# A decoder trunk on one Trainium2 core: another beginning, paired row-half matmuls, and other settings of the planner that orders the program

## The chip, the core and the metric

One core of a Trainium2 chip runs the whole kernel: TensorE (PE) multiplies, VectorE (DVE) and ScalarE (ACT) work on tiles, GpSimd (POOL) does little here, and SyncE (SP) issues the transfers from and to the chip's memory. The metric is the device time of one launch in microseconds (us), the median of the runs.

## What is computed

Two layers, each with three mixers beside each other and a gated feed-forward part, on a sequence of 256 tokens of 1024 channels. All of it is in 32-bit floating point.

```python
c_act = jax.nn.silu(c)
for l in range(DEPTH):                                  # 2
    mod = c_act @ w_ada[l] + b_ada[l]                   # 1024 x 6144
    sh1, sc1, gt1, sh2, sc2, gt2 = jnp.split(mod, 6, axis=-1)
    h = modulate(rms_norm(x, norm_mix[l]), sh1, sc1)
    p = h @ w_in[l]
    y_att = dilated_mixture_attention(q, k, v)          # 8 heads of 64
    y_rwkv = rwkv7_time_mix(p[..., i0:i1], ...)         # 8 heads of 64, low-rank decay and a
    y_gmlp = chunked_spatial_gating(p[..., i1:i2], ...)
    gates = jax.nn.sigmoid(p[..., i2:].reshape(B, S, N_BRANCH, D))
    branch = jnp.einsum('bsnw,nwd->bsnd', ys, w_branch[l])
    x = x + gt1[:, None, :] * (jnp.sum(gates * branch, axis=2) @ w_out[l])
    h = modulate(rms_norm(x, norm_ffn[l]), sh2, sc2)
    x = x + gt2[:, None, :] * conv_gated_ffn(h, ...)
return rms_norm(x, norm_final)
```

## The kernel before

**Layout.** Channels lie on the 128 partitions, tokens in the free dimension: `x` is 128 x 8 x 256, eight tiles of 128 channels. Every wide matmul is done three times with operands split into a high part, rounded to a narrower form (`hhi`, `whi`), and a remainder (`hlo`, `wlo`): high by high, high by remainder, remainder by high. The weights come as a stream of chunks of 128 x 2048, in transfers of 1024 columns into the buffers `raw`; for each, one engine makes the high part (ACT or DVE, whichever the planner picks) and DVE subtracts it to get the remainder. `load` does this, `gemm2` and its relatives multiply with them.

**The projections of c.** Each needs 128 x 1024 weights (`wada`) multiplied by the row of c. DVE does most of them in one step with a running sum, against the row `crow`, which holds c on all partitions. Four in the beginning are done by PE, against the column `ccol` (`ada_col`; `ADA_ENG` says which).

**The beginning.** `setup` loads `x`, the row of c and the vectors `vec` (which hold the column of c too), computes the root mean square of `x` (`rstd`: squares on ACT, sums on PE, a power on POOL) and makes `crow`: a matmul with a row of ones spreads the row of c over the partitions, then tanh on ACT and two steps on DVE for each half of 512. `SEQ` lists the order of the first transfers: A is weights for c, W weights of the first `START` = 6 chunks, whose columns are laid out tile by tile. `norm_h` then makes the tiles of `hhi` and `hlo`, and `gemm_side` multiplies them tile by tile into six PSUM banks.

**The mixers.** `rwkv_half` does four RWKV heads; it begins with two low-rank products, of `th` (partitions 0 to 63 of `zx`) and `xa` (64 to 127), with `lora`. `head_rsqrt` then sums squares on PE (operand `tt`), takes a power of 8 columns on POOL (`rsqrt`), spreads it into `gt` and transposes it back on PE. `attention` does for each of four pairs of heads the scores, a softmax, a transpose and the product with the values. The scores of one head use partitions 0 to 63, those of the other 64 to 127. Its PSUM ring, `at`, has two banks.

**What sets the order.** Nothing is ordered by hand. Every operation is recorded with an engine (or two to choose from), an assumed duration and what it depends on; `Plan.flush` then schedules all of them on a model of the engines, forward and backward `ROUNDS` times, keeps the round with the earliest end, and emits the instructions in that order. Each engine runs its own list in order. `ORDER` fixes the order of the chunks in the stream. PSUM banks are taken in rings (`mm` with three, `rk` with three, `at` with two).

Of the kernel before, what the change touches and what calls it, by code (L numbers as in the profile page):

```python
# [15 lines left out]
OP = mybir.AluOpType  # L16
# [30 lines left out]
for _n, _w in (("ropec", 256), ("ropes", 256), ("abias", 384), ("mdiag", 64), ("moff", 64), ("mlow", 64),  # L47
# [9 lines left out]
    ("k0 r0 v0 u0 u1 t0 t1 g20 g21 g22 g23 p20 p21 q0 q1 k1 c0 c1 r1 v1 a0 a1 g00 g01 g02 g03 p00 p01 g10 "  # L57
# [28 lines left out]
class Plan:  # L86
# [11 lines left out]
    DMA_ISSUE = 1.1  # L98
    DMA_BW = 360e3
# [103 lines left out]
    def forward(self, prio):  # L203
# [18 lines left out]
        while todo:  # L222
# [26 lines left out]
            cost = o.alts[n][1]  # L249
            if len(o.alts) > 1:  # L250
# [11 lines left out]
            if e == "SP":  # L262
                free[e] = st + 0.5
                dma = o.end = max(dma, st + self.DMA_ISSUE) + cost
            elif e == "PE":
                free[e] = o.end = self.stream(st, cost, o.work)
            else:
                if e == "ACT" and o.table and o.table != table:
                    st, table = st + 1.28, o.table
                free[e] = o.end = st + cost  # L270
# [61 lines left out]
    def flush(self):  # L332
# [11 lines left out]
        best = None  # L344
        prio = [-o.cp for o in ops]
        self.log = []
        for k in range(ROUNDS):
# [5 lines left out]
            if k == ROUNDS - 2:  # L353
                for o, n in zip(ops, best[2]):
                    o.on = n
                ends = top
# [25 lines left out]
def decoder(ctx: ExitStack, tc: tile.TileContext, xT, crow_d, cst_d, vec_d, wada, stream, small, lnrow, bsrow, out):  # L382
# [28 lines left out]
    def pe(mms, main=False):  # L411
        cost, work, outs, ins, half = 0.0, 0.0, [], [], None
        for m in mms:
# [3 lines left out]
            was, half = half, (o.ap[0][1] == 64 and divmod(o.offset, o.ap[0][0])[0] or 0, o.ap[0][1] == 64)  # L417
            if was is not None and was[1] and half[1] and was[0] != half[0]:
# [5 lines left out]
            elif a.dtype == F32R:  # L424
                cost += max(_n(b) / 2400 + 0.0112, 0.112)
            else:
                cost += 2 * max(_n(b) / 1200 + 0.003, 0.1115)
# [182 lines left out]
    def load():  # L610
# [5 lines left out]
        for h in range(2):  # L616
# [4 lines left out]
            sub(lo, src, hi.bitcast(F32))  # L621
# [86 lines left out]
    def rsqrt(xc, y, t):  # L708
        P.add("POOL", 0.5, lambda: nc.gpsimd.tensor_tensor(y, xc, minus_half.to_broadcast(list(xc.shape)), op=OP.pow),  # L709
# [89 lines left out]
    def rwkv_half(l, hf, W, lora, th, xa, sg, yhi, ylo):  # L799
# [44 lines left out]
        pw = bank()  # L844
        pe([(bnc(pw, i), lora[0:64, (n0 + i) * 128:(n0 + i + 1) * 128], th[0:64, :], True, True) for i in range(2)])
        for i in range(2):
            act(sig[:, i, :], bnc(pw, i), AF.Tanh, scale=0.5, bias=dv[:, l, 14 + n0 + i:15 + n0 + i])
        ts(sig, sig, 0.5, 0.5, OP.mult, OP.add)
        pa = bank()
        pe([(bnc(pa, i), lora[64:128, (n0 + i) * 128:(n0 + i + 1) * 128], xa[64:128, :], True, True)  # L850
            for i in range(2)])
# [221 lines left out]
    def attention(l, W, yhi, ylo):  # L1073
# [120 lines left out]
    def setup(W):  # L1194
        tmp, wide2 = W["m3"], W["m2"]
        P.boost = 4000.0
        for j in range(4):
            dma(x[:, 2 * j:2 * j + 2, :], xT[:, 2 * j:2 * j + 2, :])
        dma(tmp[0:1, :], crow_d)
        dma(vec, vec_d)  # L1200
        memset(wide2[0:1, 0:128], 1.0)
        for n in range(2):
            ps = bank("mm")
            pe([(ps, wide2[0:1, 0:128], tmp[0:1, n * 512:(n + 1) * 512], True, True)])
            c = slice(n * 512, (n + 1) * 512)
# [6 lines left out]
        mul(ccol, tc, ccol)  # L1212
        for l in range(L):
# [272 lines left out]
def _pack(i):  # L1486
# [41 lines left out]
    return {"xT": xT, "crow": np.asarray(i["c"]), "cst": _constants(), "vec": vec, "wada": wada, "stream": stream, "small": small,  # L1528
# [19 lines left out]
```

## Time and profile before

| | |
|---|---|
| median of 3 runs | 1061.46 us (1059.19 to 1063.53) |
| the profiled execution | 1065.56 us |
| its span, first to last instruction | 1063.8 us |
| read from memory, written | 212.12 MB, 4.19 MB |
| mean rate over the span | 203 GB/s |
| granted TensorE clock, mean | 0.981 |

A profile row has a start, a duration, the engine, the line and the operation, then output<-inputs by the program's names, the shapes and a count; in brackets the idle time of the engine just before it and what ended that. Matmuls are pipelined: a row's duration is longer than the time until the next may start. A row that covers several instructions runs from the first one's start to the last one's end. A 32-bit matmul that isn't split stands as two records. In rows of waits the numbers are us in total, times, and the longest. In rows of stages: the stretch and its length, then busy us (instructions) of PE, weight load, DVE, ACT and POOL, the granted clock, the DMA engines' busy share and GB/s; where a view is of one engine, its columns alone.

### The profile page before, as it was taken

The page shows a single profiled execution, that of the slowest core. Times are in us where ns is not written, and L with a number is a line of the kernel's source. Part 1 is how long each engine was busy: PE and PEld are TensorE (multiplying, and loading weights), DVE is VectorE, ACT ScalarE, POOL GpSimd, SP SyncE. Part 2 cuts the span into 40 slices and gives each one's busy share as a digit, 9 for nine tenths or more (in the row PEclk, how much of TensorE's full clock was granted, in tenths as well). Part 3 has the DMA queues.
Part 4 walks back from the last instruction along what each step waited for, and adds up shares of the span by engine and source line. Part 5 has one row for each costly group of instructions (what it writes and reads, how often), then busy time and mean ns, then how long its engine had stood idle before and what let it go on. Part 6 is the DMA issues. An engine that isn't in the chain of part 4 may idle for free. (4 is left out here: it accounts for less than half of the span.)

```text
span 1063.8 us, 20460 instructions
## 1 busy us (share of the span) xinstructions
PE 1008.1 (95%) x8042; PEld 968.8 (91%) x8042; DVE 896.0 (84%) x1820; ACT 526.9 (50%) x917; POOL 34.4 (3%) x27
## 2 busy tenths in 40 slices
PE   5999998899999999999999999889999999999996
PEld 4989997689889999999999899879899999999996
DVE  6979999889769899999999799679976789877753
ACT  4364456656434555544436645455643465343341
POOL 0010000100000000000010100010000000000000
PEclk9999999899999899999999999999999999999998
DMA  9888565364578668988995454415434646555541
GB/s 350 322 279 264 190 210 185 118 203 162 186 257 275 201 218 299 315 287 279 380 314 191 146 163 138 157 34 182 134 118 136 217 143 207 190 181 187 185 143 40
DMA packets 70130, 217.65 MB, mean 205 GB/s; under 512 B 15121, under 2 KB 17169, under 8 KB 69522
## 3 DMA queue, kind: packets, MB, share of 16 engines
q1 hardware_dynamic: 70034, 216.35, 60.8%
q8 instruction: 63, 1.03, 0.4%
q14 instruction: 33, 0.27, 0.1%
HBM read 212.12 MB, written 4.19 MB: 203 GB/s over the span
## 5 line engine op out<-in xcount | busy, mean ns | idle before, releaser
L434 PE MATMUL bkm<-hhi,whi 128*128 128x256 f32 x1104 | 322.0, 292 | 5.2 <-DVE m L462 4.0
L462 DVE TENSOR_TENSOR wlo<-raw,whi 128x1024 fp32r<-128x1024 f32 x235 | 285.7, 1220 | 43.5 <-ACT whi L458 42.5
L434 PE MATMUL bkm<-hlo,whi 128*128 128x256 f32 x1104 | 314.5, 285 | 1.6 <-DVE hlo L495 1.6
L434 PE MATMUL bkm<-hhi,wlo 128*128 128x256 f32 x1104 | 314.0, 284 | 0.0
L458 ACT CAST whi<-raw 128x1024 fp32r<-128x1024 f32 x198 | 206.8, 1047 | 214.8 <-PE bkm L434 105.8
L434 PEld LDWEIGHTS bkm<-hhi,whi 128*128 128x128 f32 x1104 | 213.3, 193 | 11.8 <-issue 10.3
L434 PEld LDWEIGHTS bkm<-hlo,whi 128*128 128x128 f32 x1104 | 213.6, 193 | 2.4 <-DVE hlo L495 2.0
L434 PEld LDWEIGHTS bkm<-hhi,wlo 128*128 128x128 f32 x1104 | 213.4, 193 | 0.0
L434 PE MATMUL bkr<-hhi,whi 128*128 128x256 f32 x368 | 104.5, 284 | 0.0
L434 PE MATMUL bkr<-hlo,whi 128*128 128x256 f32 x368 | 104.5, 284 | 0.0
L434 PE MATMUL bkr<-hhi,wlo 128*128 128x256 f32 x368 | 104.4, 284 | 0.0
L434 PEld LDWEIGHTS bkr<-hhi,whi 128*128 128x128 f32 x368 | 71.1, 193 | 0.0
L434 PEld LDWEIGHTS bkr<-hlo,whi 128*128 128x128 f32 x368 | 71.0, 193 | 0.0
L434 PEld LDWEIGHTS bkr<-hhi,wlo 128*128 128x128 f32 x368 | 71.0, 193 | 0.0
L495 DVE SCALAR_TENSOR_TENSOR bd<-bd,crow 128x1024 f32<-128x1024 f32 x52 | 63.3, 1220 | 5.2 <-DMA bd<-in_wada_dram 5.0
L462 DVE TENSOR_TENSOR wlo<-m,whi 128x1024 fp32r<-128x1024 f32 x45 | 54.9, 1220 | 14.0 <-ACT whi L458 13.8
L458 ACT CAST whi<-m 128x1024 fp32r<-128x1024 f32 x39 | 40.8, 1047 | 49.2 <-PE bkm L434 23.3
L709 POOL TENSOR_TENSOR rs<-rs,vec 128x8 f32<-128x8 f32 (+2 forms) x17 | 23.4, 1377 | 766.8 <-DVE rs L482 668.6
L434 PE MATMUL bkm<-ygh,whi 128*128 128x256 f32 (+1 forms) x156 | 46.4, 298 | 0.6 <-ACT ygh L458 0.4
L434 PE MATMUL bkm<-ygl,whi 128*128 128x256 f32 x156 | 44.6, 286 | 1.7 <-DVE ygl L462 1.6
L434 PE MATMUL bkm<-ygh,wlo 128*128 128x256 f32 (+1 forms) x156 | 44.2, 284 | 0.0
L495 DVE SCALAR_TENSOR_TENSOR raw<-raw,crow 128x1024 f32<-128x1024 f32 x34 | 41.2, 1218 | 3.6 <-DMA raw<-in_wada_dram 3.6
(520 smaller groups left out, 2203.4 us busy)
## 6 DMA issues: line engine op xcount, KB each, us to landing
raw<-in_stream_dram SPq DMA_DIRECT2D x238, 512.0 KB, 4.7
bd<-in_wada_dram SPq DMA_DIRECT2D x52, 512.0 KB, 5.9
m<-in_stream_dram SPq DMA_DIRECT2D x47, 512.0 KB, 4.8
raw<-in_wada_dram SPq DMA_DIRECT2D x34, 512.0 KB, 5.1
m<-in_wada_dram SPq DMA_DIRECT2D x7, 512.0 KB, 8.7
scx<-x SPq DMA_DIRECT2D x2, 1024.0 KB, 10.0
x<-scx SPq DMA_DIRECT2D x2, 1024.0 KB, 7.0
x<-in_xT_dram SPq DMA_DIRECT2D x4, 256.0 KB, 4.2
```

The source lines that it names most:

```text
L434: nc.tensor.matmul(m[0], m[1], m[2], start=m[3], stop=m[4], skip_group_check=len(m) > 5)
L458: P.either([("ACT", _act(a), lambda: nc.scalar.copy(o, a)), ("DVE", 0.07 + _n(a) / (960 if _psum(o, a) else 1920), lambda: nc.vector.tenso ...
L462: P.add("DVE", 0.07 + _n(a) / 960, lambda: nc.vector.tensor_tensor(o, a, b, op=op), [o], [a, b])
L495: P.add("DVE", c, lambda: nc.vector.scalar_tensor_tensor(o, a, s, b, op0=op0, op1=op1, **k), [o, accum], ins)
L709: P.add("POOL", 0.5, lambda: nc.gpsimd.tensor_tensor(y, xc, minus_half.to_broadcast(list(xc.shape)), op=OP.pow), [y], [xc, minus_half])
```

## The change

The row of c is no longer loaded. The column of c goes through the same tanh form as before, and eight transposes of its entries, each spread over 128 columns, give the row, which is copied out of PSUM in two halves. `SEQ` is generated: for each channel tile its two A transfers, then the W transfers up to that tile. The two low-rank products of an RWKV half and the scores of two heads are recorded as one group each, with the two row halves in turn. The planner's settings: 100 rounds with random shifts of the end times instead of 12, other assumed costs for transfers, for matmuls of 64 rows, and for the power on POOL (0.6, 1.65 or 2.65 us by width instead of 0.5), and a rule by which DVE holds back an operation of over 0.5 us if a much more urgent one is ready within 0.15 us. The remainders of chunks 6 to 34 are made in halves of 512 columns. In layer 0, chunk g20 stands ahead of t0 and t1.

```diff
-    ("k0 r0 v0 u0 u1 t0 t1 g20 g21 g22 g23 p20 p21 q0 q1 k1 c0 c1 r1 v1 a0 a1 g00 g01 g02 g03 p00 p01 g10 "
+    ("k0 r0 v0 u0 u1 g20 t0 t1 g21 g22 g23 p20 p21 q0 q1 k1 c0 c1 r1 v1 a0 a1 g00 g01 g02 g03 p00 p01 g10 "
...
-SEQ = [(_a[0], int(_a[1]), int(_a[2])) for _a in (
-    "A01 W00 W01 A00 A10 A20 W10 W11 A21 A11 W20 A31 A30 A40 W21 A41 "
-    "A60 A51 A50 W30 W31 A61 W40 A71 W41 W50 W51 A70"
-).split()]
-ROUNDS = 12
+SEQ = []
+for _k in range(8):
+    SEQ += [("A", _k, 0), ("A", _k, 1)]
+    SEQ += [("W", _d // 2, _d % 2) for _d in range(-(-_k * START // 4), -(-(_k + 1) * START // 4))]
+ROUNDS, SEED = 100, 1
+FINE = 35
+HOLD, SHORT, WAIT, URGENT = ("DVE",), 0.5, 0.15, 10.0
...
-    DMA_ISSUE = 1.1
-    DMA_BW = 360e3
+    DMA_ISSUE = 1.75
+    DMA_BW = 340e3
...
+            if e in HOLD and cost > SHORT:
+                near = [x for x in w if not x[3].done and x[0] <= st + WAIT and prio[x[1]] < prio[o.i] - URGENT]
+                if near:
+                    heapq.heappush(a, (prio[o.i], o.i, n, o))
+                    free[e] = min(x[0] for x in near)
+                    continue
...
-                free[e] = st + 0.5
+                free[e] = st + 0.4
...
-            if k == ROUNDS - 2:
+            if k > 8:
                 for o, n in zip(ops, best[2]):
                     o.on = n
-                ends = top
+                s = (0.3, 1.0, 1.0, 3.0)[k % 4]
+                ends = [e + rng.gauss(0.0, s) for e in top]
...
-            was, half = half, (o.ap[0][1] == 64 and divmod(o.offset, o.ap[0][0])[0] or 0, o.ap[0][1] == 64)
-            if was is not None and was[1] and half[1] and was[0] != half[0]:
+            was, half = half, [(y.ap[0][1] == 64, divmod(y.offset, y.ap[0][0])[0]) for y in (o, a)]
+            if was is not None and any(p[0] and q[0] and p[1] != q[1] for p, q in zip(was, half)):
                 cost, half = cost + 0.035, None
...
-                cost += max(_n(b) / 2400 + 0.0112, 0.112)
+                cost += max(_n(b) / 2400 + 0.0125, 0.112)
...
-                cost += 2 * max(_n(b) / 1200 + 0.003, 0.1115)
+                cost += 2 * max(_n(b) / 1200 + 0.003, 0.1115) + (0.097 if a.ap[0][1] == 64 and _n(b) > 128 else 0.0)
...
-            sub(lo, src, hi.bitcast(F32))
+            for q in (slice(0, 512), slice(512, 1024)) if i < FINE else (slice(0, 1024),):
+                sub(lo[:, q], src[:, q], hi[:, q].bitcast(F32))
...
-        P.add("POOL", 0.5, lambda: nc.gpsimd.tensor_tensor(y, xc, minus_half.to_broadcast(list(xc.shape)), op=OP.pow),
+        P.add("POOL", {1: 0.6, 2: 1.65, 8: 2.65}[_n(xc)], lambda: nc.gpsimd.tensor_tensor(y, xc, minus_half.to_broadcast(list(xc.shape)), op=OP.pow),
...
-        pw = bank()
-        pe([(bnc(pw, i), lora[0:64, (n0 + i) * 128:(n0 + i + 1) * 128], th[0:64, :], True, True) for i in range(2)])
+        pw, pa = bank(), bank()
+        pe([(bnc(p, i), lora[h, (n0 + i) * 128:(n0 + i + 1) * 128], r[h, :], True, True)
+            for i in range(2) for p, h, r in ((pw, H[0], th), (pa, H[1], xa))])
...
-        pa = bank()
-        pe([(bnc(pa, i), lora[64:128, (n0 + i) * 128:(n0 + i + 1) * 128], xa[64:128, :], True, True)
-            for i in range(2)])
...
-            for hs in H:
-                ps = bank("at")
-                pe([(ps[:, 0:128], q[hs, n, 0:128], k[hs, n, 0:128], True, True),
-                    (ps[:, 128:384], q[hs, n, 128:256], k[hs, n, :], True, True)])
+            pss = [bank("at") for _ in H]
+            pe([x for c, kc in ((0, 128), (128, 256)) for ps, hs in zip(pss, H)
+                for x in [(ps[:, c:c + kc], q[hs, n, c:c + 128], k[hs, n, 0:kc], True, True)]])
+            for ps in pss:
...
+        dma(vec, vec_d)
         for j in range(4):
             dma(x[:, 2 * j:2 * j + 2, :], xT[:, 2 * j:2 * j + 2, :])
-        dma(tmp[0:1, :], crow_d)
-        dma(vec, vec_d)
-        memset(wide2[0:1, 0:128], 1.0)
-        for n in range(2):
-            ps = bank("mm")
-            pe([(ps, wide2[0:1, 0:128], tmp[0:1, n * 512:(n + 1) * 512], True, True)])
-            c = slice(n * 512, (n + 1) * 512)
-            act(crow[:, c], ps, AF.Tanh, scale=0.5)
-            ts(crow[:, c], crow[:, c], 1.0, 0.5, OP.add, OP.mult)
-            mul(crow[:, c], ps, crow[:, c])
...
         mul(ccol, tc, ccol)
+        for n in range(2):
+            ps = bank("mm")
+            pe([(ps[:, k * 128:(k + 1) * 128], ccol[:, 4 * n + k:4 * n + k + 1].to_broadcast([128, 128]), ident)
+                for k in range(4)])
+            acopy(crow[:, n * 512:(n + 1) * 512], ps)
```

Three places in the instructions' order follow, word for word, for PE. The first is its beginning, before: sq are squares of `x`, m_0 the row of c and the ones, vec holds the column of ones, the identity and the column of c, and VK and PB are here weights for c.

```order
L434 MATMUL bkm_93<-m_0_138,m_0_137 128x512
L434 MATMUL bkm_94<-m_0_138,m_0_137 128x512
L434 MATMUL bka_99<-vec,sq_108 128x1 x4
L434 MATMUL bka_99<-vec,sq_109 128x1 x2
L432 MATMUL bka_100<-vec,rs_90 128x128 x2
L434 MATMUL bka_99<-vec,VK_141 128x1 x8
L434 MATMUL bka_100<-vec,PB_140 128x1 x8
L434 MATMUL bkm_95<-hhi,whi_79 128x256
```

And with the change (m_115 are weights for c):

```order
L444 MATMUL bka_99<-vec,sq_108 128x1 x4
L442 MATMUL bkm_93<-vec 128x128 x4
L444 MATMUL bka_99<-vec,sq_109 128x1 x2
L442 MATMUL bkm_94<-vec 128x128 x4
L442 MATMUL bka_100<-vec,rs_90 128x128 x2
L444 MATMUL bka_99<-vec,m_115 128x1 x8
L444 MATMUL bka_100<-vec,VK_141 128x1 x8
L444 MATMUL bkm_94<-hhi,whi_79 128x256
```

The one-row matmuls are gone, the square sums stand first, and the eight transposes stand between them.

The second place is the start of the second RWKV half of layer 0, before: zx,lora are the low-rank products, tt the squares, gt what comes back from POOL.

```order
L434 MATMUL bka1_100<-m01_115 128x128
L434 MATMUL bka1_100<-m01_115 128x256
L432 MATMUL bkr0_96<-vec_66,kkn_1_156 128x128 x4
L434 MATMUL bkr2_98<-zx_1_158,lora_120 128x256 x2
L434 MATMUL bkr0_96<-cst_65,tt_1_157 128x2 x4
L432 MATMUL bkr1_97<-vec_66,gt_1_155 128x128 x4
L434 MATMUL bkm2_95<-whi2_81,hhi_75 128x512
```

With the change, its first rows:

```order
L444 MATMUL bkr1_97<-zx_1_158,lora_120 128x256
L444 MATMUL bkr2_98<-zx_1_158,lora_120 128x256
L444 MATMUL bkr1_97<-zx_1_158,lora_120 128x256
L444 MATMUL bkr2_98<-zx_1_158,lora_120 128x256
L444 MATMUL bkr0_96<-cst_65,tt_1_157 128x2 x4
L444 MATMUL bkm2_95<-hhi_75,whi1_80 128x256
L444 MATMUL bkm2_95<-hlo_76,whi1_80 128x256
L444 MATMUL bkm2_95<-hhi_75,wlo1_84 128x256
```

After 24 rows of wide matmuls of that kind (the last of them is the first row here) it goes on:

```order
L444 MATMUL bkm2_95<-hhi_75,wlo1_84 128x256
L442 MATMUL bka0_99<-vec_66,m3_0_138 128x128 x3
L442 MATMUL bka1_100<-vec_66,s21_1_160 128x128 x3
L442 MATMUL bkr1_97<-vec_66,gt_1_155 128x128 x4
L444 MATMUL bkm2_95<-whi2_81,hhi_75 128x512
```

Between the sums (tt) and the transposes (gt) there was nothing; now there are 24 wide matmuls and six transposes of the attention. The low-rank products, which stood in two groups apart, alternate between their two banks.

The third place is the same chain in the first RWKV half of layer 1, with the change:

```order
L444 MATMUL bkr1_97<-cst_65,tt_3_186 128x2 x4
L444 MATMUL bkm2_95<-hhi_75,whi0_79 128x256
L444 MATMUL bkm2_95<-hlo_76,whi0_79 128x256
L444 MATMUL bkm2_95<-hhi_75,wlo0_83 128x256
L444 MATMUL bkm2_95<-hhi_75,whi0_79 128x256
L444 MATMUL bkm2_95<-hlo_76,whi0_79 128x256
L444 MATMUL bkm2_95<-hhi_75,wlo0_83 128x256
L444 MATMUL bkm2_95<-hhi_75,whi0_79 128x256
L444 MATMUL bkm2_95<-hlo_76,whi0_79 128x256
L444 MATMUL bkm2_95<-hhi_75,wlo0_83 128x256
```

Three more wide matmuls follow and then the transposes of gt: 12 matmuls stand there now, where before 22 wide ones and four low-rank ones stood.

More of the change, by code (lines that the diff above doesn't have):

```diff
@@ L2 @@
 import math
+import random
 from contextlib import ExitStack
@@ L343, in flush @@
             o.cp = m + (o.cost + (self.DMA_ISSUE if o.eng == "SP" else 0.0)) * o.w + o.b
-        best = None
+        best, rng = None, random.Random(SEED)
         prio = [-o.cp for o in ops]
@@ L381, in decoder @@
 @with_exitstack
-def decoder(ctx: ExitStack, tc: tile.TileContext, xT, crow_d, cst_d, vec_d, wada, stream, small, lnrow, bsrow, out):
+def decoder(ctx: ExitStack, tc: tile.TileContext, xT, cst_d, vec_d, wada, stream, small, lnrow, bsrow, out):
     nc = tc.nc
@@ L1194, in setup @@
     def setup(W):
-        tmp, wide2 = W["m3"], W["m2"]
         P.boost = 4000.0
+        dma(vec, vec_d)
         for j in range(4):
             dma(x[:, 2 * j:2 * j + 2, :], xT[:, 2 * j:2 * j + 2, :])
-        dma(tmp[0:1, :], crow_d)
-        dma(vec, vec_d)
-        memset(wide2[0:1, 0:128], 1.0)
-        for n in range(2):
-            ps = bank("mm")
-            pe([(ps, wide2[0:1, 0:128], tmp[0:1, n * 512:(n + 1) * 512], True, True)])
-            c = slice(n * 512, (n + 1) * 512)
-            act(crow[:, c], ps, AF.Tanh, scale=0.5)
-            ts(crow[:, c], crow[:, c], 1.0, 0.5, OP.add, OP.mult)
-            mul(crow[:, c], ps, crow[:, c])
         tc = acol[:, 0:8]
@@ L1527, in _pack @@
     bsrow = np.ascontiguousarray(i["gmlp_b_s"])
-    return {"xT": xT, "crow": np.asarray(i["c"]), "cst": _constants(), "vec": vec, "wada": wada, "stream": stream, "small": small,
+    return {"xT": xT, "cst": _constants(), "vec": vec, "wada": wada, "stream": stream, "small": small,
             "lnrow": lnrow, "bsrow": bsrow}
```

## The prediction

> **What bounds the kernel now.** I read the engine table of the page first, then busy time by stage, then the list of waits of TensorE (PE), and then the order of time around the waits that the change touches.
>
> ```profile
> span 1063.8 us, 20460 instructions
> PE 1008.1 (95%) x8042; PEld 968.8 (91%) x8042; DVE 896.0 (84%) x1820; ACT 526.9 (50%) x917; POOL 34.4 (3%) x27
> ```
>
> The stages, by busy time of PE, weight load, VectorE (DVE), ScalarE (ACT) and GpSimd (POOL): the beginning, the mixers of layer 0, its feed-forward part, the same two of layer 1, and the end.
>
> ```profile
> 0.00:24.78 24.78, 13.57 (x51) 10.96 (x51) 16.23 (x47) 11.10 (x20) 1.88 (x5) 1.00 0.91 346
> 24.78:355.00 330.22, 307.02 (x2404) 288.88 (x2404) 287.95 (x624) 169.18 (x311) 14.76 (x9) 0.97 0.67 222
> 355.00:554.50 199.50, 198.03 (x1624) 197.83 (x1623) 194.23 (x372) 101.65 (x159) 4.32 (x3) 0.98 0.83 287
> 554.50:842.30 287.80, 276.32 (x2184) 258.34 (x2184) 237.11 (x514) 152.94 (x282) 12.05 (x9) 0.99 0.45 146
> 842.30:1054.50 212.20, 212.17 (x1779) 212.09 (x1779) 157.75 (x262) 91.55 (x146) 0.70 (x1) 1.00 0.51 167
> ```
>
> The feed-forward stages are solid PE (198.03 of 199.50, 212.17 of 212.20): nothing that moves other engines' work can shorten them, save for a reduced clock. 1779 matmuls in 212.2 us also give the price of one: 0.119 us. What can be won lies in the first 24.78 us and in the two mixer stages, where PE stands idle 23.2 us (330.22 - 307.02) and 11.5 us (287.80 - 276.32). DVE has 288 of 330 us there in layer 0, so it is the next bound. The idle spots have a second price:
>
> ```profile
> 201.07:211.30 10.23, 6.31 (x16) 0.50 0.32 103
> 166.90:170.30 3.40, 3.40 (x17) 0.50 0.50 144
> 354.70:364.90 10.20, 10.20 (x48) 0.50 0.72 242
> ```
>
> Behind some waits the granted clock is 0.50 for 3.4 or 10.2 us, and PE work in it counts half: 6.31 busy us cost about 3.2 us more than at full clock.
>
> **Part 1, the beginning.** Today's row of c comes by two one-row matmuls, tanh, and two DVE steps for each half:
>
> ```profile
> 7.56 3.75 PE L434 MATMUL bkm<-m,m 1*128 1x512 f32 x4 [7.56 <-DMA m<-in_crow_dram]
> 8.80 0.20 ACT L452 ACTIVATE acol<-vec 128x8 f32<-128x8 f32 x1
> 9.32 0.16 DVE L462 TENSOR_TENSOR vec<-acol,vec 128x8 f32<-128x8 f32 x1
> 9.63 0.60 ACT L452 ACTIVATE crow<-bkm 128x512 f32<-128x512 f32 x1 [0.63 <-PE bkm L434]
> 11.23 2.72 PE L434 MATMUL bka<-vec,sq 128*128 128x1 f32 x12
> 15.05 0.68 DVE L462 TENSOR_TENSOR crow<-bkm,crow 128x512 f32<-128x512 f32 x1
> 15.88 1.67 POOL L709 TENSOR_TENSOR rs<-rs,vec 128x2 f32<-128x2 f32 x1 [15.44 <-DVE rs L482]
> 17.61 0.69 PE L432 MATMUL bka<-vec,rs 128*128 128x128 f32 x2 [3.65 <-POOL rs L709]
> 18.09 3.41 PE L434 MATMUL bka<-vec,VK 128*128 128x1 f32 x16
> 21.36 3.55 PE L434 MATMUL bka<-vec,PB 128*128 128x1 f32 x16
> 24.78 0.56 PE L434 MATMUL bkm<-hhi,whi 128*128 128x256 f32 x1
> ```
>
> The row is whole at 15.73, and the square sums (vec,sq) stand behind the one-row matmuls on PE. The changed kernel needs the column of c, ready at 9.48 today (9.32 + 0.16). PE's rows are then four square sums, four transposes, two square sums, four transposes. A square sum is two of the twelve records, so 0.45 us (2.72 / 6): four take 1.8, from 8.85 (vec is there) to 10.65. A transpose costs 0.14 to 0.35 us (the pair at 17.61 took 0.69, PE took up the next work 0.48 after its start); at the small end, with a copy of 0.60 on ACT, the row is whole at about 13.5, 2.2 us sooner. The square sums end near 12; then DVE's short step, POOL 1.67, two transposes: about 14.9 instead of 18.3. PE next runs two projections of c (8 matmuls, 16 records, 3.41 us each), whose weights are the 11th and 13th of the transfers. The 13th is VK in both kernels and is there by 18.09 today, the 11th two transfers of 512 KB earlier; at the 408 GB/s below that is 2.6 us, so 15.5. PE: 15.5 to 18.9, then VK to 22.2, then the first projection matmul: **2.6 us** sooner than 24.78. DVE must have finished its first tile by then: from 13.5 the order gives it five steps of 1024 columns (1.2 us each) and shorter ones, 7 us together, 20.5, so it isn't late.
>
> ```profile
> 20.00:30.00 10.00, 10.00 (x48) 10.00 (x48) 9.86 (x21) 6.09 (x9) 0.00 (x0) 1.00 1.03 408
> ```
>
> Here PE (10.00), DVE (9.86) and the DMA engines (1.03) are all full. So an earlier start of PE counts as long as neither of the others makes it wait, and both do the same work as today. The transfers' new order on SP's queue moves no byte but the 4 KB of c, so the last weight lands as today. Bounds: 0, if a weight of the second or third tile is now the late one; 4, if the projections' weights are earlier than I infer.
>
> **Part 2, paired matmuls of 64 rows.** In the low-rank products (zx,lora) and the attention scores (bka<-m with 64 rows) the kernel multiplies one half of the partitions and then the other.
>
> ```profile
> 65.61 1.13 PE L434 MATMUL bkr<-zx,lora 64*128 64x256 f32 x4
> 66.67 1.05 PE L434 MATMUL bkr<-cst,tt 128*128 128x2 f32 x8
> 192.93 0.92 PE L434 MATMUL bka<-m 64*128 64x128 f32 x4
> 193.69 0.38 PE L434 MATMUL bkr<-zx,lora 64*128 64x256 f32 x1
> 223.64 0.27 PE L434 MATMUL bka<-s,m 128*64 128x128 f32 x1
> 223.64 0.27 PE L434 MATMUL bka<-m,m 128*64 128x128 f32 x1
> 223.75 0.27 PE L434 MATMUL bka<-s,m 128*64 128x128 f32 x1
> ```
>
> One group of the first kind holds PE for 1.06 us (65.61 to 66.67), one score group 0.76 (192.93 to 193.69). No row shows two halves of rows at once. Column halves do run together: the two at 223.64 start in the same hundredth, the next pair follows 0.11 later, the time of one. Bounds: 0 if row halves don't overlap, and 4 x 1.06 + 8 x 0.76 = 10.3 us if they do wholly (4 RWKV halves, 8 pairs of heads in two layers). I take the column pairs as nearest, and four fifths of it, **8.2**, since parts of the mixer stages are held by DVE.
>
> The Trainium skill, "TensorE: Matmul & The Clock Gate", part 3, says that matmuls in different row groups run at the same time; that would give the 10.3. Its "TensorEngine Tiling (Array Packing)", gotcha 1, speaks against: row tiles must not use one PSUM bank at once, so pairing costs banks. Here the scores of two heads take both banks of their ring together; no run yet shows the price.
>
> **Part 3, the new order around long chains.** In the chain behind the sums tt, POOL raises 8 columns to a power:
>
> ```profile
> 201.54 2.49 POOL L709 TENSOR_TENSOR rs<-rs,vec 128x8 f32<-128x8 f32 x1 [4.92 <-DVE rs L482]
> 204.06 0.62 ACT L458 COPY gt<-rs 128x512 f32<-128x512 f32 x1 [1.71 <-POOL rs L709]
> 204.73 1.12 PE L432 MATMUL bkr<-vec,gt 128*128 128x128 f32 x4 [3.97 <-ACT gt L458]
> PE bkr L432 <- ACT gt L458: 7.9, 3, 4.0
> PE bkr L432 <- DVE kkn L462: 1.9, 2, 1.7
> 354.56 0.72 PE L434 MATMUL bka<-vec,sq 128*128 128x1 f32 x3 [2.15 <-DVE sq L462]
> ```
>
> The planner counts 0.5 us for it now, 2.65 after the change. By the rows of the order, 11, 0, 26 and 18 wide matmuls stand between sums and transposes now (four low-rank ones among the 26); 58, 30 (six of them transposes), 12 and 42 after. The chain leaves PE 3.97 us with no cover. At 0.119 us, 58 and 42 cover it; 30 leave 0.4; 12 leave 2.5. So 7.9 us of idle time become 2.9: 5.0 gained. The second chain, to kkn, goes from 18, 36, 22 and 54 to 60, 48, 48 and 78: its 1.9 us become at most 0.2, 1.7 gained. With the 3.97 us goes most likely the half clock at 201.07 to 211.30, 3.2. Together **9.9**. At the end of the mixers of layer 0, six matmuls now stand ahead of vec,sq: **0.7** of the 2.15. The matmuls that cover are taken from elsewhere; where, no trace shows. I leave every other wait as it is; bounds -10 (new waits as long as those gone) and +14 (half of the other 25 us of mixer idle time goes too, and a little clock).
>
> **Part 4, remainders in halves.** 58 remainders of 1024 columns become 116 of 512.
>
> ```profile
> 45.16 0.68 DVE L462 TENSOR_TENSOR zr<-raw,zk 128x512 fp32r<-128x512 f32 x1
> 45.76 0.68 DVE L462 TENSOR_TENSOR aa<-raw,sig 128x512 fp32r<-128x512 f32 x1
> 47.05 1.23 DVE L462 TENSOR_TENSOR wlo<-raw,whi 128x1024 fp32r<-128x1024 f32 x1
> 48.20 1.22 DVE L462 TENSOR_TENSOR wlo<-m,whi 128x1024 fp32r<-128x1024 f32 x1
> ```
>
> By starts, two halves take 2 x 0.60 against 1.15: 0.05 more, 3 us in all; by durations 2 x 0.68 against 1.22: 0.14, 8 us. All of it falls in layer 0's mixers, where DVE is 87% busy. PE hides what it can as long as DVE isn't late; I take **-2** between 0 and -8. The gain is that PE may start on a first half 0.6 us earlier.
>
> **Sum.** 2.6 + 8.2 + 9.9 + 0.7 - 2 = 19.4 us. The profiled execution took 1065.56 (1063.8 of span, 1.8 around it): 1046.2. The median of the runs, 1061.46, is 4.1 lower, so the forecast is **1042**.
>
> **Rivals.**
> 1. The planner finds more: half of the other idle time goes too (+14) and pairs overlap wholly (+2): 1026. For it: waits of 4.03 and 2.04 us remain whose half clock would go with them. Against: DVE is at 87% and gets more work.
> 2. Pairing gives nothing: row halves run in turn, or the score groups wait for their two banks what they saved. 1042 + 8 = 1050. For it: the ring of the scores has two banks alone; against: the column pairs above, which gain in that ring.
> 3. The change doesn't do what it says in part 3: the cover is taken from places that then wait as long. Without 10.6 of the sum: 1053; with rival 2's loss too, 1061, no change.
> 4. Slower: DVE becomes the bound of layer 0's mixers and PE finds its PSUM banks not emptied, as once today:
>
> ```profile
> 166.78 0.42 PE L434 MATMUL bkm<-hhi,whi 128*128 128x256 f32 x1 [4.03 <-DVE m L462]
> ```
>
> That wait with its 3.4 us at half clock costs 4.03 + 1.7 = 5.7 us. Five new ones (28.5) outweigh the sum and give 1042 + 28.5 = 1071; from five on it is slower.
>
> **Chances.** Forecast 0.54 (1034 to 1048 by itself), rival 1 0.15, rival 2 0.11, rival 3 0.12 (half of it no change), rival 4 0.08. The range runs from 1024, below rival 1, to 1058, above 1053. A measurement of this kernel tells about 0.5% from no change: faster means below 1056, slower above 1067. Faster 0.54 + 0.15 + 0.11 + 0.06 = 0.86, the same 0.06, slower 0.08.
>
> **What would show it.** First hhi,whi matmul near 22 us; if it is at 24 or later, part 1 fell. Two zx,lora groups in about 1.1 us together instead of 2.1, and rows of both halves starting together; else part 2 fell. No wait on gt near the second RWKV half of layer 0 and clock 1.00 behind it, but one of 2 to 3 us in the first half of layer 1; else part 3 fell. Mixer stages of about 317 and 284 us (13 and 3.5 of the sum fall there). If the feed-forward stages change by more than 5 us, something is at work that I haven't seen.

## The result, and the profile after

The changed kernel takes 1034.17 us (median of 4 runs, 1032.91 to 1036.74) against 1061.83 for the kernel before in the same runs (1059.19 to 1063.53): the ratio is 0.9745, 95% interval [0.9715, 0.9774]. That is 27.7 us, where 19.4 were forecast. The engine table of the changed kernel's page:

```profile
span 1034.9 us, 20493 instructions
PE 987.6 (95%) x8046; PEld 954.2 (92%) x8046; DVE 905.1 (87%) x1911; ACT 517.2 (50%) x881; POOL 40.3 (4%) x27
```

For the stages, both kernels are now cut at two events that are in both: the first projection matmul, and the transposes that end the root mean square of `x` after each part. First the beginning, mixers, feed-forward part, mixers, feed-forward part of the kernel before; the columns are those of the stage rows above.

```profile
0.00:24.78 24.78, 13.57 (x51) 10.96 (x51) 16.23 (x47) 11.10 (x20) 1.88 (x5) 1.00 0.91 346
24.78:364.93 340.15, 316.95 (x2449) 298.81 (x2450) 296.17 (x637) 173.73 (x318) 16.38 (x10) 0.96 0.67 223
364.93:557.98 193.05, 191.58 (x1600) 191.38 (x1600) 188.47 (x365) 98.39 (x153) 4.32 (x3) 1.00 0.84 291
557.98:868.01 310.03, 298.55 (x2377) 280.57 (x2377) 254.28 (x542) 163.25 (x300) 11.13 (x8) 0.99 0.46 148
868.01:1056.41 188.40, 187.07 (x1570) 186.90 (x1568) 138.38 (x226) 80.12 (x127) 0.70 (x1) 1.00 0.49 160
```

The same view of the changed kernel:

```profile
0.00:23.66 23.66, 11.90 (x55) 11.16 (x55) 13.67 (x43) 9.04 (x18) 1.06 (x5) 1.00 0.90 338
23.66:344.97 321.31, 304.35 (x2449) 287.51 (x2450) 296.65 (x697) 172.73 (x313) 15.84 (x10) 0.99 0.70 233
344.97:537.13 192.16, 192.12 (x1613) 191.90 (x1612) 191.18 (x379) 91.26 (x132) 2.51 (x2) 1.00 0.83 284
537.13:839.89 302.76, 292.37 (x2372) 277.31 (x2371) 263.07 (x567) 163.55 (x291) 20.18 (x9) 0.98 0.51 162
839.89:1027.54 187.65, 186.32 (x1564) 186.15 (x1563) 138.04 (x224) 80.24 (x129) 0.69 (x1) 1.00 0.50 159
```

The beginning gives 1.1 us, the mixers of layer 0 18.8, those of layer 1 7.3, the two feed-forward parts 0.9 and 0.75. In layer 0 the granted clock tells most: 0.96 before, 0.99 after. Before, 27.3 us of that stage ran at half clock, and PE was busy in 23.4 of them; after, 3.4, all of them busy. If PE work at half clock counts half, that alone is 10.0 us. PE's idle time there fell from 23.2 (340.15 - 316.95) to 17.0, another 6.2, and the 2.6 that are left are less PE work. In layer 1 idle time gave 1.1 us (11.5 to 10.4) and the clock took 0.6 (4.9 to 6.1 busy us at half clock), so 6.8 us there are less PE work. Added up from the first projection matmul to the end of the last stage shown, in us:

| | PE's idle time | half of the busy time at half clock | PE work at full clock |
|---|---|---|---|
| before | 37.5 | 15.1 | 979.1 |
| changed kernel | 28.7 | 4.8 | 970.4 |

So 8.8 us came from idle time, 10.3 from the clock and 8.7 from less PE work.

The beginning, in order of time on PE in the changed kernel:

```profile
13.69 0.69 PE L442 MATMUL bka<-vec,rs 128*128 128x128 f32 x2 [0.24 <-POOL rs L720]
16.84 3.55 PE L444 MATMUL bka<-vec,m 128*128 128x1 f32 x16 [2.46 <-DMA m<-in_wada_dram]
20.24 3.55 PE L444 MATMUL bka<-vec,VK 128*128 128x1 f32 x16
23.66 0.56 PE L444 MATMUL bkm<-hhi,whi 128*128 128x256 f32 x1
```

The transposes of the root mean square come at 13.69 instead of 17.61, more than hoped for. Then PE waits 2.46 us for weights of c, which land at 16.84 and not at 15.5. What had been a wait for POOL is now a wait for a transfer.

The products of 64 rows, PE's groups by shape (busy us, mean ns of one), first before, then after:

```profile
L434 PE MATMUL bka<-m 64*128 64x256 f32 x32 | 9.5, 377 | 0.0
L434 PE MATMUL bkr<-zx,lora 64*128 64x256 f32 x32 | 8.9, 399 | 0.0
L434 PE MATMUL bka<-m 64*128 64x128 f32 x32 | 7.7, 319 | 0.5 <-DVE m L462 0.5
```

```profile
L444 PE MATMUL bka<-m 64*128 64x256 f32 x32 | 5.4, 382 | 0.0
L444 PE MATMUL bka<-m 64*128 64x128 f32 x32 | 4.7, 322 | 0.1
L444 PE MATMUL bkr<-zx,lora 64*128 64x256 f32 x32 | 4.5, 401 | 1.1 <-ACT hhi L468 1.1
```

One matmul takes as long as before, and the three rows' busy times add up to 26.1 us before and 14.6 after. The scores' two rows overlap a little, so some time is counted twice in that sum; the time in which any 64-row matmul runs falls from 23.2 to 12.7 us, by 10.5. The row halves do run beside each other.

PE's waits after the change, the longest groups among the mixers':

```profile
PE bkr L442 <- ACT gt L468: 6.1, 2, 4.1
PE bkr L442 <- DVE sig L472: 4.8, 2, 3.9
PE bkm L444 <- DVE hlo L472: 2.5, 2, 1.8
```

The waits on `gt` are one of 2.0 us in the second half of layer 0 and one of 4.1 in the first half of layer 1. The other two chain ends have no wait. The cover that was forecast (58, 30, 12 and 42 wide matmuls) is there, and two of four places wait, as forecast, but the second one for longer, for a reason that the section on the hardware looks into. The waits on `sig` stand under DVE, but most of the longest, 3.9 us, is a wait for a transfer, for which DVE itself waited:

```profile
152.71 0.69 DVE L472 TENSOR_TENSOR sig<-Tc,cst 128x512 f32<-128x512 f32 x1 [2.54 <-DMA Tc<-scb]
```

So not all of what the table below puts down to DVE is its own.

### The profile page after: what moved, and what is told of

Its sections match the earlier page's. It is cut to its first block, busy times and chain, and to the rows that moved or that the text cites. A ratio compares the mean times of both kernels' runs of the same rounds, so it can differ in the third digit from the quotient of the medians.

```text
span 1034.9 us, 20493 instructions
## 1 busy us (share of the span) xinstructions
PE 987.6 (95%) x8046; PEld 954.2 (92%) x8046; DVE 905.1 (87%) x1911; ACT 517.2 (50%) x881; POOL 40.3 (4%) x27
## 5 line engine op out<-in xcount | busy, mean ns | idle before, releaser
L468 ACT CAST whi<-raw 128x1024 fp32r<-128x1024 f32 x205 | 214.4, 1048 | 237.6 <-PE bkm L444 118.8
L472 DVE TENSOR_TENSOR wlo<-raw,whi 128x1024 fp32r<-128x1024 f32 (+1 forms) x293 | 293.0, 1008 | 33.9 <-ACT whi L468 32.5
L444 PEld LDWEIGHTS bkr<-hhi,wlo 128*128 128x128 f32 x368 | 70.6, 192 | 0.3 <-DVE wlo L472 0.3
L444 PEld LDWEIGHTS bkr<-hhi,whi 128*128 128x128 f32 x368 | 70.6, 192 | 0.0
L444 PEld LDWEIGHTS bkr<-hlo,whi 128*128 128x128 f32 x368 | 70.6, 192 | 0.0
L468 ACT CAST whi<-m 128x1024 fp32r<-128x1024 f32 x38 | 39.8, 1047 | 47.6 <-PE bkm L444 18.9
L720 POOL TENSOR_TENSOR rs<-rs,vec 128x8 f32<-128x8 f32 (+2 forms) x17 | 29.0, 1709 | 714.3 <-DVE rs L492 714.3
## 6 DMA issues: line engine op xcount, KB each, us to landing
m<-in_wada_dram SPq DMA_DIRECT2D x6, 512.0 KB, 10.2
```

What stands on the lines that cost most here:

```text
L444: nc.tensor.matmul(m[0], m[1], m[2], start=m[3], stop=m[4], skip_group_check=len(m) > 5)
L468: P.either([("ACT", _act(a), lambda: nc.scalar.copy(o, a)), ("DVE", 0.07 + _n(a) / (960 if _psum(o, a) else 1920), lambda: nc.vector.tenso ...
L472: P.add("DVE", 0.07 + _n(a) / 960, lambda: nc.vector.tensor_tensor(o, a, b, op=op), [o], [a, b])
L720: P.add("POOL", {1: 0.6, 2: 1.65, 8: 2.65}[_n(xc)], lambda: nc.gpsimd.tensor_tensor(y, xc, minus_half.to_broadcast(list(xc.shape)), op=OP. ...
```

## The experiments

Most edits are planned anew, so they also draw another order. The runs below give the size of that. Each ratio is to runs of the kernel before on the same chip; the kernels ran on several chips, so small differences between them are better read from the ratios. In the table, "PE waits" are the waits of PE after the first projection matmul, summed over the list of waits, with those that DVE ended in brackets; "half clock" is the time at 0.50 in the mixers and feed-forward stages; both are of one profiled execution, in us.

| kernel | median us | ratio to before, 95% interval | PE waits (on DVE) | half clock |
|---|---|---|---|---|
| before | 1061.83 | 1 | 37.0 (22.4) | 34.1 |
| before + pairs | 1059.18 | 0.9986 [0.9962, 1.0009] | 45.5 (29.9) | 30.7 |
| before + DVE's rule | 1060.16 | 0.9978 [0.9959, 0.9996] | 31.4 (20.9) | 30.7 |
| before + all settings | 1051.37 | 0.9905 [0.9874, 0.9936] | 28.9 (17.3) | 17.1 |
| before + all settings + pairs | 1034.68 | 0.9742 [0.9718, 0.9766] | 26.2 (17.5) | 17.4 |
| **changed kernel** | 1034.17 | 0.9745 [0.9715, 0.9774] | 27.2 (12.0) | 13.6 |
| halves of rows not in turn | 1035.23 | 0.9732 [0.9697, 0.9767] | 25.2 (12.8) | 20.4 |
| remainders whole | 1035.26 | 0.9733 [0.9699, 0.9766] | 28.3 (13.6) | 10.2 |
| POOL's cost 0.5 | 1038.93 | 0.9759 [0.9719, 0.9798] | 27.2 (13.3) | 6.9 |
| loop of 12 rounds | 1033.63 | 0.9734 [0.9679, 0.9790] | 24.7 (17.6) | 13.6 |
| pairs undone | 1037.64 | 0.9791 [0.9751, 0.9830] | 21.4 (10.2) | 10.2 |
| DVE's rule undone | 1047.29 | 0.9875 [0.9832, 0.9919] | 31.6 (23.0) | 30.7 |
| the same, another seed | 1045.33 | 0.9838 [0.9819, 0.9857] | 27.9 (15.4) | 17.1 |
| DVE's rule with 0.30 us | 1028.09 | 0.9679 [0.9657, 0.9701] | 18.3 (12.9) | 10.2 |

**Row halves one after the other.** The order of the plan stays; within each group the matmuls of the second half of rows come after those of the first.

```diff
+        seq = mms
+        if all(len(m) > 3 and m[1].ap[0][1] == 64 for m in mms):
+            seq = sorted(mms, key=lambda m: divmod(m[1].offset, m[1].ap[0][0])[0])
...
-            for m in mms:
+            for m in seq:
```

> The changed kernel with its order of instructions kept, but in each group of paired 64-row matmuls the one row half stands wholly before the other. Theory (the two halves overlap in full and TensorE sets the pace): the trace of the changed kernel has 0.97 us for a low-rank group of both halves and 0.76 us for a score group; in turn they take up to twice that, less one matmul that still overlaps where the halves meet, so 4 x 0.8 + 8 x 0.6 = 8 us more: 1042, all of it in the two mixer stages. Rival (the order has slack, or another engine sets the pace there): under 3 us more, 1037 or less.

1035.23, no change, but not for the reason given there. The first low-rank group in the order of time on PE, in this kernel:

```profile
67.39 1.14 PE L448 MATMUL bkr<-zx,lora 64*128 64x256 f32 x8
```

Its eight records take 1.14 us, as after the change, not twice as long. They start in twos, 13 ns apart, although the two of a pair stand four records apart in the program. So this edit took nothing away, and the run says nothing of what the overlap is worth. What brings the halves together again, the records, which don't name the half, don't show.

**Remainders whole.** The plan stays; the remainder of 1024 columns is made in one step at the place of the first half.

```diff
-                sub(lo[:, q], src[:, q], hi[:, q].bitcast(F32))
+                o = sub(lo[:, q], src[:, q], hi[:, q].bitcast(F32))
+                if i < FINE:
+                    o.alts[0] = ("DVE", o.alts[0][1], (lambda: None) if q.start else (
+                        lambda lo=lo, src=src, hi=hi: nc.vector.tensor_tensor(lo, src, hi.bitcast(F32), op=OP.subtract)))
```

> The changed kernel with its order kept, but each remainder of chunks 6 to 34 made in one piece of 1024 columns at the place of its first half. Theory (the halves cost VectorE 0.05 to 0.14 us each and win nothing that the trace shows): 0 to 3 us less, 1031 to 1034. Rival (TensorE really starts on first halves 0.6 us earlier, and waits without it): 2 to 6 us more, 1036 to 1040, with new waits of TensorE on wlo.

1035.26: the halves cost nothing and give nothing. DVE's groups by shape show the price that is hidden, 116 halves in the changed kernel, and the 58 whole remainders in this one (the third row):

```profile
L472 DVE TENSOR_TENSOR wlo<-raw,whi 128x1024 fp32r<-128x1024 f32 x177 | 215.3, 1220 | 30.0 <-ACT whi L468 29.0
L472 DVE TENSOR_TENSOR wlo<-raw,whi 128x512 fp32r<-128x512 f32 x116 | 77.7, 684 | 3.8 <-ACT whi L468 3.5
```

```profile
L635 DVE TENSOR_TENSOR wlo<-raw,whi 128x1024 fp32r<-128x1024 f32 x58 | 70.6, 1219 | 6.0 <-ACT whi L468 5.9
```

77.7 against 70.6 us of DVE, 7.1 more, and the mixers of layer 0 are not longer for it (321.31 against 320.11 whole). This kernel, the one before it and the changed kernel share one order, and yet have 10.2, 20.4 and 13.6 us at half clock: so much can differ between two executions of one order.

**POOL's power at the old cost.**

```diff
-        P.add("POOL", {1: 0.6, 2: 1.65, 8: 2.65}[_n(xc)], lambda: nc.gpsimd.tensor_tensor(y, xc, minus_half.to_broadcast(list(xc.shape)), op=OP.pow),
+        P.add("POOL", 0.5, lambda: nc.gpsimd.tensor_tensor(y, xc, minus_half.to_broadcast(list(xc.shape)), op=OP.pow),
```

> The changed kernel planned with the old duration of 0.5 us for the power on GpSimd. Theory (the honest duration is what put cover behind the sums): the cover falls below 34 matmuls at several of the four places, TensorE waits there 2 to 4 us each and gets half clock behind some: 6 to 12 us more, 1040 to 1046. Rival (the many rounds of the search matter, not this number): within 3 us of the changed kernel.

1038.93; its interval overlaps that of the changed kernel, and its profiled span is 1032.9. All four chain ends wait again (1.2, 2.6, 1.2 and 1.6 us on `gt`), so the cost does what it says there, but the whole hardly moves: 1.5 us by the ratios, as the rival has it.

**The old loop of 12 rounds.**

```diff
-ROUNDS, SEED = 100, 1
+ROUNDS, SEED = 12, 1
...
-            if k > 8:
+            if k == ROUNDS - 2:
...
-                s = (0.3, 1.0, 1.0, 3.0)[k % 4]
-                ends = [e + rng.gauss(0.0, s) for e in top]
+                ends = top
```

> The changed kernel planned with the old loop: 12 rounds and no random shifts; costs, pairs and the beginning as changed. Theory (costs and pairs matter most): 2 to 8 us more, 1036 to 1042. Rival (the search itself is the larger part of the gain): 10 us more or beyond, 1044 and up.

1033.63: the longer search is worth nothing that shows. The orders of the last two runs and that of the changed kernel (which the first two runs share) end between 1033.6 and 1038.9, so 5 us is what a newly drawn order may do at the least, and less than that can't be put down to an edit here.

**Pairs undone.** Each half of rows is a group again.

```diff
-        pw, pa = bank(), bank()
-        pe([(bnc(p, i), lora[h, (n0 + i) * 128:(n0 + i + 1) * 128], r[h, :], True, True)
-            for i in range(2) for p, h, r in ((pw, H[0], th), (pa, H[1], xa))])
+        pw = bank()
+        pe([(bnc(pw, i), lora[0:64, (n0 + i) * 128:(n0 + i + 1) * 128], th[0:64, :], True, True) for i in range(2)])
...
-            pss = [bank("at") for _ in H]
...
+            for hs in H:
+                ps = bank("at")
...
```

> The changed kernel with the low-rank products and the scores recorded as before, each row half as a group of its own (one PSUM bank of the scores' ring at a time). Theory P (the two row halves side by side are worth 8 to 10 us, as forecast): 1042 to 1045 us, 8 to 10 above the changed kernel, and the mixers of layer 0 and 1 longer by about 5 and 4. Theory S (the scheduler's settings carry the gain, the pairs little): 1034 to 1038.

1037.64, in the range of theory S. The time of the groups is back, by shape:

```profile
L444 PE MATMUL bka<-m 64*128 64x256 f32 x32 | 9.5, 377 | 0.0
L444 PE MATMUL bkr<-zx,lora 64*128 64x256 f32 x32 | 9.0, 401 | 0.4 <-ACT zx L462 0.4
L444 PE MATMUL bka<-m 64*128 64x128 f32 x32 | 7.8, 322 | 0.2 <-DVE m L505 0.2
```

26.3 us instead of 14.6. But this order has 5.8 us fewer waits (21.4 against 27.2) and starts its first projection matmul at 19.4, with one of the projections of c (3.4 us) put behind it. So 11.7 us of PE work show as 3.5 us of time (4.9 by the ratios), within what a new order may do.

**DVE's rule undone.**

```diff
-HOLD, SHORT, WAIT, URGENT = ("DVE",), 0.5, 0.15, 10.0
+HOLD, SHORT, WAIT, URGENT = (), 0.5, 0.15, 10.0
```

> The changed kernel without the rule by which DVE holds back a long operation for a more urgent one. Theory H (the rule carries a third or more of the 27 us): 1043 us or more, with new waits of PE on short DVE steps (kkn, s, sq) in the mixers of layer 0. Theory P or S without it: 1032 to 1037, within the scatter of a re-drawn order.

1047.29: 13 us, the largest of all single edits. That is theory H's number, but the longest waits are not those it named. The waits of PE on DVE:

```profile
PE bkr L442 <- DVE sig L472: 9.8, 4, 4.5
...
PE bkr L444 <- DVE BK L472: 2.4, 2, 1.8
...
PE bkr L442 <- DVE yrh L472: 1.8, 1, 1.8
...
PE bkm L444 <- DVE zv L505: 1.5, 1, 1.5
```

And its mixers of layer 0, with two of the stretches at half clock in them:

```profile
24.27:357.30 333.03, 312.00 (x2455) 294.75 (x2456) 299.09 (x709) 172.67 (x312) 19.55 (x10) 0.96 0.68 227
...
164.92:175.16 10.24, 8.69 (x54) 7.33 (x52) 10.05 (x22) 4.52 (x10) 0.00 (x0) 0.50 0.48 155
199.05:209.29 10.24, 8.78 (x30) 6.66 (x30) 9.88 (x23) 4.28 (x11) 1.69 (x1) 0.50 0.34 116
```

The stage is 11.7 us longer than after the change, at the old granted clock of 0.96: 4.1 us more idle time, 10.4 more for the clock (24.3 busy us at half clock against 3.4) and 2.8 less PE work. The waits on DVE are 23.0 us instead of 12.0, as many as before the change (22.4); all waits together rise by 4.4.

**Pairs alone, and the settings alone**, on the kernel before; the lines are those of the change's diff, of which a few are shown. Pairs:

```diff
-            was, half = half, (o.ap[0][1] == 64 and divmod(o.offset, o.ap[0][0])[0] or 0, o.ap[0][1] == 64)
+            was, half = half, [(y.ap[0][1] == 64, divmod(y.offset, y.ap[0][0])[0]) for y in (o, a)]
...
+        pw, pa = bank(), bank()
...
+            pss = [bank("at") for _ in H]
...
```

> The kernel before with the pairs alone, and the planner's recognition of them. Theory P: 1052 to 1054, 8 to 10 below the kernel before. Theory S: 1059 to 1063, the same as before. Theory X: 1056 to 1062, since the old costs leave the idle spots where they are.

Settings, with the costs of matmuls of 64 rows and of POOL's power:

```diff
-ROUNDS = 12
+ROUNDS, SEED = 100, 1
+HOLD, SHORT, WAIT, URGENT = ("DVE",), 0.5, 0.15, 10.0
...
-    DMA_ISSUE = 1.1
-    DMA_BW = 360e3
+    DMA_ISSUE = 1.75
+    DMA_BW = 340e3
...
```

> The kernel before with the planner's settings alone (100 rounds, the rule for DVE, the costs of transfers, of matmuls of 64 rows and of POOL's power); beginning, chunk order, pairs and remainders as before. Theory S (settings carry the gain): 1036 to 1044, 18 to 26 below the kernel before. Theory P (pairs carry 8 to 10, the settings about 10 as forecast): 1050 to 1053. Theory X (it is the pieces together, none alone): 1056 or more.

The pairs alone leave the time where it was, 0.9986 [0.9962, 1.0009]: their groups fall from 26.1 to 16.4 us, and PE's waits rise from 37.0 to 45.5. The settings alone give 0.9905 [0.9874, 0.9936], some 10 us.

**Settings and pairs together, and DVE's rule alone**, on the kernel before (the first has the edits of both runs above, the second only the line with HOLD and the rule).

> The kernel before with the planner's settings and the pairs; beginning, chunk order and remainders as before. If the two add up (work -9 by the pairs, losses -14 by the settings): 1040 to 1043, work 994, and the beginning and g20 are worth the other 6 to 8. If the rest of the change is worth no more than its first matmul (about 1): 1033 to 1037. If the pairs gain nothing on this base, as nearly on the old one: 1048 to 1052.

> The kernel before with DVE's rule alone (12 rounds, old costs, no pairs). So far PE's full-clock work (span less idle time less half of the half-clock time) is 1002 to 1004 without pairs and 992 to 994 with them, and idle plus lost clock is 61 before, 42 after, 54 after without the rule. Theory H (the rule by itself keeps PE from waiting): 1048 to 1052, losses near 49, work 1003. Rival C (the rule works only with the right costs): 1058 to 1063, losses 57 or more.

Together they give all of it: 0.9742 [0.9718, 0.9766], against 0.9745 [0.9715, 0.9774] for the whole change. The first projection matmul is at 25.06 in that kernel, 1.4 us later than after the change, and the end is the same; on top of the settings and the pairs, the new beginning, g20 and the halves add nothing that can be measured. The pairs gain 16.7 us on the settings, where they gained next to nothing without them. But the changed kernel with its pairs undone, which has the settings and these three pieces, ends 13.7 us below the settings alone (1037.64 against 1051.37, on the same chip). Either the pieces count where the pairs are missing, or one of these two orders is an uncommon draw, and then a new draw can do far more than 5 us; no run decides it. So 16.7 is no price of the pairs.

What the pairs do in every order is to take PE work away. Reckoned at full clock as in the table of the result, it is 967 to 973 us in the ten kernels with pairs, and 979 to 981 in the four without (where a projection of c stands behind the first projection matmul, its 3.4 us are taken off). The settings act on the rest: idle time and clock, 52.6 us before, are 37.7 with the settings alone, 34.4 with the pairs too and 33.5 after the change.

DVE's rule alone gives 0.9978 [0.9959, 0.9996], some 2 us: its worth also hangs on the rest.

**DVE's rule undone, from another seed.**

```diff
-ROUNDS, SEED = 100, 1
+ROUNDS, SEED = 100, 2
...
-HOLD, SHORT, WAIT, URGENT = ("DVE",), 0.5, 0.15, 10.0
+HOLD, SHORT, WAIT, URGENT = (), 0.5, 0.15, 10.0
```

> The changed kernel without DVE's rule, as e8, from another seed: another draw of the order. Theory H (the rule is worth about 12): 1042 to 1050. Rival D (e8 was an unlucky draw): 1033 to 1038, as the four orders with the rule.

1045.33: two orders without the rule at 1045 and 1047, four with it and with the pairs at 1034 to 1039 (the changed kernel, POOL's cost 0.5, 12 rounds, settings and pairs). The rule is the likely cause of the 11 to 13 us between them (10 to 14 by the ratios), but with 1051 for the settings alone, which have the rule, two unlucky draws can't be ruled out. Where this second order loses it is less plain than in the first: its waits are 27.9 us, like the changed kernel's, of them 15.4 on DVE, where settings and pairs have 17.5 with the rule, and its half clock is 17.1. One thing both share: POOL's first power of 8 columns, which the first RWKV half of layer 0 needs, starts at 74.05 and 73.79 us, and at 63.4 to 69.6 in every order with the rule.

**The rule with 0.30 us instead of 0.15.**

```diff
-HOLD, SHORT, WAIT, URGENT = ("DVE",), 0.5, 0.15, 10.0
+HOLD, SHORT, WAIT, URGENT = ("DVE",), 0.5, 0.3, 10.0
```

> The changed kernel with DVE holding a long step back for an urgent one that is ready within 0.30 us instead of 0.15. Theory H: the same or a little less, 1028 to 1036, losses 38 to 42. Rival (0.15 just hit a good order): 1038 or more.

1028.09 (1027.80 to 1029.13), ratio 0.9679 [0.9657, 0.9701], clear of the changed kernel's interval (each against the kernel before, on other chips): this version beats both. Its page, and its two mixer stages:

```profile
span 1025.9 us, 20483 instructions
PE 987.3 (96%) x8046; PEld 954.2 (93%) x8046; DVE 896.6 (87%) x1894; ACT 523.0 (51%) x898; POOL 34.3 (3%) x27
```

```profile
24.99:342.43 317.44, 306.55 (x2455) 290.45 (x2456) 294.01 (x695) 173.84 (x315) 16.11 (x10) 0.98 0.70 235
...
533.51:830.99 297.48, 291.01 (x2379) 275.59 (x2378) 258.10 (x560) 169.76 (x301) 13.11 (x9) 1.00 0.52 167
```

3.9 and 5.3 us shorter than after the change; its waits are 18.3 us, the fewest of all. No wait on `gt` is left in it, 6.1 us in the changed kernel, nor the half clock of 10.24 us around the longer of these: the power that is slow there (the last section tells of it) takes 1.68 us in this order. It is one order, so how much is the setting and how much the order is open.

## Why the prediction was right, and where not

The time fell in the range, 7.8 us below the forecast. Sorted by what PE did, the forecast had 7.4 us of idle time (5.0 + 1.7 + 0.7), 3.2 of clock, 8.2 of PE work, 2.6 of beginning and -2 for DVE. Between the two profiled executions it was 8.8, 10.3, 8.7, 1.1 and nothing that shows. So the term that was mis-sized is the clock, by 7 us, and the other errors nearly cancel. That the idle time came out near its term is in part luck: of the 5.0 at `gt` only 1.8 came, and other waits went in their place.

- **Part 1, 2.6 us: measured 1.1 at the first projection matmul, nothing at the end.** The row of c was whole at 14.1 instead of 13.5. The error is in "15.5" for the weights of c: they landed at 16.84. And the old beginning in a kernel that is otherwise alike ends at the same time (1034.68 against 1034.17), so "an earlier start of PE counts" is not borne out either.
- **Part 2, 8.2 us: the mechanism was right.** Row halves overlap wholly: the time in which a 64-row matmul runs fell by 10.5 us (23.2 to 12.7), just over the upper bound of 10.3, and PE work by 8.7. The step from PE time to run time was too simple: the same saving brought some 1.5 us on the old settings, 16.7 on the new ones, and 3.5 when undone in the changed kernel, since each time other waits moved.
- **Part 3, 9.9 us: right in its places, wrong in its cause and its size.** The covers are there, but 2.0 and 4.1 us of waits were left for `gt` where 0.4 and 2.5 were forecast: 1.8 us gained there instead of 5.0. The wait before vec,sq, of which 0.7 were to go, went whole (2.15). But with POOL's cost back at 0.5 the time rises by no more than a new order may add. The step that failed is "I leave every other wait as it is", and with it the clock: 3.2 us were forecast, for one stretch, and the half-clock time of the stages fell from 34.1 to 13.6 us, worth 10.3 (7.0 and 12.0 in the two other runs of the same order). DVE's rule, which got no term of its own, is the likely cause of a large part: without it the changed kernel takes 11 to 13 us more. How it works is shown in one order only, where the waits on DVE and the half clock go back to their old sizes (23.0 and 30.7); in the other they don't (15.4 and 17.1).
- **Part 4, -2 us: nothing.** DVE works 7.1 us more, inside the bounds of 3 to 8, and PE hides all of it. Rival 4, DVE as the bound, did not come.
- **Feed-forward stages:** 0.9 and 0.75 us, inside the 5 that the forecast allowed.
- **The mixer stages** are 18.8 and 7.3 shorter, where 13 and 3.5 were forecast. In layer 0 idle time and clock explain 16.2 of the 18.8, and 2.6 are less PE work; in layer 1 it is 6.8 of the 7.3. The 64-row matmuls run some 5 us less in each of the two. Why the layers differ, the trace, whose ends of matmuls are modelled, doesn't settle.

So the result is half rival 1 (the planner finds more), probably by a setting that I read as a detail.

## What to carry to other kernels

Where a planner draws the order, a saving in engine time becomes a saving in time only as far as the waits let it: price an edit on both the old and the new base, and first measure how much a newly drawn order alone moves the time (here 5 us at the least). On the engine that serves the bound one, a short urgent step that misses its turn behind a long one can cost its wait and, on top, half clock behind it; a rule by which the planner lets that engine stand for up to 0.15 us was the edit whose loss cost most here. Look for the settings that act on every step before those that act on four.

## What the runs showed of the hardware

**A power on POOL took 7.02 us, where most take 1.6 to 2.5.** In order of time, first half of layer 1 of the changed kernel:

```profile
549.23 7.02 POOL L720 TENSOR_TENSOR rs<-rs,vec 128x8 f32<-128x8 f32 x1 [14.10 <-DVE rs L492]
...
551.27 3.49 DVE L472 TENSOR_TENSOR wlo<-raw,whi 128x1024 fp32r<-128x1024 f32 x3
...
556.29 0.62 ACT L468 COPY gt<-rs 128x512 f32<-128x512 f32 x1 [4.02 <-POOL rs L720]
...
556.96 1.12 PE L442 MATMUL bkr<-vec,gt 128*128 128x128 f32 x4 [4.11 <-ACT gt L468]
```

ACT takes up the result only at 556.29, so the duration is real. From 549.33 to 554.76 DVE runs without a break, seven subtractions with two inputs from the on-chip memory and three casts with one, and the power ends 1.49 us after that. The two other runs of the same order show 7.03 and 7.02 (row halves not in turn, remainders whole). Two other orders show the same: in the kernel with the settings alone DVE runs on to 565.00 and the power ends at 566.49,

```profile
558.66 7.83 POOL L718 TENSOR_TENSOR rs<-rs,vec 128x8 f32<-128x8 f32 x1 [13.61 <-DVE rs L491]
```

and in the first kernel without the rule a power of 4.36 us ends at 78.41, 1.50 us after DVE's first break at 76.91. In the kernel with 0.30 us the power in question stands beside a one-input step and a scan of two inputs, and is short, although DVE runs on there too:

```profile
545.74 1.68 POOL L720 TENSOR_TENSOR rs<-rs,vec 128x8 f32<-128x8 f32 x1 [13.62 <-DVE rs L492]
```

The Trainium skill, "SBUF — State Buffer", section "SBUF: two separate sides", says that DVE and GpSimd share a pair of ports as an exclusive lock, and that a DVE operation with two inputs from that memory takes it against a GpSimd operation that reads there. The rows agree in part: the long powers lie beside such subtractions, but the scan did not hold the power up. That the lock is the cause was not tried by itself.

**Matmuls of two row halves overlapped in both orders tried.** With the halves one after the other in the program, they start in twos 13 ns apart (the group of 1.14 us above); in turn, 7 ns.

**Half clock does not go by the length of the wait.** In the kernel with 0.30 us, waits of 1.41 and 1.82 us are each followed by 3.41 us at half clock:

```profile
90.65 0.58 PE L444 MATMUL bkm<-hhi,whi 128*128 128x256 f32 x1 [1.41 <-ACT m L462]
...
266.77 0.66 PE L442 MATMUL bkr<-vec,sig 128*128 128x128 f32 x4 [1.82 <-DVE sig L472]
```

```profile
90.60:94.01 3.41, 3.36 (x15) 3.36 (x16) 2.45 (x8) 3.40 (x6) 0.00 (x0) 0.50 0.89 241
...
268.09:271.50 3.41, 3.41 (x24) 3.08 (x24) 2.29 (x5) 0.57 (x2) 0.00 (x0) 0.50 0.71 215
```

In the changed kernel one of 2.01 us is followed by none:

```profile
195.97 0.66 PE L442 MATMUL bkr<-vec,gt 128*128 128x128 f32 x4 [2.01 <-ACT gt L468]
...
```

```profile
194.00:204.00 10.00, 7.71 (x36) 6.28 (x37) 9.96 (x19) 8.39 (x15) 0.00 (x0) 1.00 0.40 132
```

So a wait's second price, up to 1.7 us (half of 3.41), or up to 5.1 for the stretches of 10.24, can only be counted as likely, not as certain. Nor does half clock need a wait: in the kernel with the settings alone PE has no idle time for 8 us ahead of this stretch, but 32 records of matmuls of one column.

```profile
37.35 1.84 PE L443 MATMUL bka<-vec,m 128*128 128x1 f32 x16
39.05 1.93 PE L443 MATMUL bka<-vec,BK 128*128 128x1 f32 x16
```

```profile
41.54:44.95 3.41, 3.41 (x19) 0.50 0.53 213
```

That these matmuls bring it about is not shown.
